# Strassen's seven half-size products in pairs of column blocks after the attention, with operand sums, and gates and branch results kept in DRAM

## The chip, the core and the metric

The kernel runs on one core of one Trainium2 chip. Its engines are TensorE (PE in the profile: matrix products), VectorE (DVE), ScalarE (ACT), GpSimd (POOL) and SyncE (SP, which here only starts DMAs). The metric is the device time of one launch in microseconds (us). The kernel before took 1020.76 us, the median of three runs (1018.58 to 1023.02).

## The reference

One layer on 1024 frames of 1024 channels, all in float32. Cut to what matters here:

```python
h = x @ w_in          # q, k, v, gate_a, alpha_low, pool_in, gate_b, merge_logits
o = gated_linear_attention(q, k, v, log_alpha)          # 4 heads, chunks of 64 frames
y_a = norm(o) * gla_norm_g * silu(gate_a)
y_b = pooled_and_mixed(pool_in, w_pool_grp) * pool_scale * silu(gate_b)
g_a, g_b = split(sigmoid(merge_logits + b_merge))
merged = g_a * (y_a @ w_proj_a) + g_b * (y_b @ w_proj_b)
return layernorm(ALPHA * x + merged @ w_out) * ln_g + ln_b
```

`pooled_and_mixed` takes, per group of 256 channels, a trailing mean over 2, 4, 8 or 16 frames minus the frame itself, and a 256 by 256 product. Every other product named here is 1024 deep.

## The kernel before, in words

**Products.** A float32 operand is held as an exact pair of two reduced-precision (fp32r) parts, hi and lo, and a product is hi·hi + hi·lo + lo·hi. `split` (L49) makes a pair: ACT casts hi (L50), DVE subtracts lo = src − hi (L51). A column block is 128 output columns for all 1024 frames: `acc_gen` (L101) runs 8 blocks of depth times 3 parts times 2 halves of 512 frames, 48 instructions of 128x512 (L112), into a PSUM tile of two banks (`ps_acc`, two such tiles). The weights of a block come in one 512 KB load into `raw` and are split in two pieces of 128x512.

**Stages.** After the loads come the v, q, k and decay products, then the attention, head after head (L470 to L515). Between the attention's steps `fill` (L453) runs products that do not depend on it; the last of them are the eight blocks of the merge logits of branch A (`la`), whose raw results go to DRAM (`la_d`). From then on the order is that of the code: per pool group two `pi` blocks (the pooling input), two `gb` blocks (the gate) and a small mix `mx`; then `lb` (merge gate b) and `pb` (projection b) in turn; then `gta` (gate a, times the attention's output, read back from DRAM); then `pa` (projection a, gated, plus branch B's result `mb`); then `out` (L638, the product with w_out), the residual and the layernorm. Each is eight column blocks, `out` eight frame blocks in two halves. The operands stay in SBUF: x (`xh`, `xl`), y_b and later y_a (`yh`, `yl`), merged (`mh`, `ml`), w_out (`wo0`, `wo1`), the gates and `mb`.

**What sets the order.** Each engine runs its own queue in order and waits for the others by semaphores. The queues follow the order in which the code issues the work; a block under `tc.high_priority(offset=...)` is placed that much earlier. All DMAs of this kernel are started from SP's one queue, and a DMA that waits holds up those behind it there. A tile of a pool waits until the earlier user of its buffer is done.

**Who does what after the attention.** PE runs the products. DVE makes the lo parts, the gating products (L565, L579, L593, L613), the pooling sums, the residual and the layernorm. ACT makes the hi parts, the gates and PSUM copies. POOL does eight additions of `mb` (L614) and the power of the layernorm's root (L415).

## Time and profile before

| | us |
|---|---|
| median of three runs | 1020.76 |
| profiled execution, first to last instruction (span) | 1019.1 |
| PE busy | 993.6 |
| DVE busy | 498.5 |
| ACT busy | 287.9 |
| POOL busy | 111.7 |

The profiled execution's own time is told by its span; the median of the runs lies 1.7 us above that, which is taken as what lies around the span. PE is busy 98% of it. The stages after the attention begin in the trace at 378.7 us (`pi`, `gb`, `mx`), 575.2 (`lb`, `pb`), 749.1 (`gta`), 836.2 (`pa`) and 923.2 (`out`); the last product ends at 1011. "Idle before" in a group of instructions is the time the engine stood still ahead of them, and the name behind the arrow is what it then waited for.

### The profile page before, as it was taken

Reading aid. Unit: us, or ns where it says so; the run is one execution under the profiler, and the core shown is the slowest. Engines: PE = TensorE matmul, PEld = TensorE weight load, DVE = VectorE, ACT = ScalarE, POOL = GpSimd, SP = SyncE. Lnnn points to the kernel's source line nnn. Section 1 sums busy time; section 2 is a strip of 40 time slices with the busy share of each in tenths; the row PEclk is TensorE's granted clock in tenths of the full one; section 3 lists DMA queues with packets and bytes.
Section 4 is the critical chain, followed back from the end, with each engine's and each line's share of the span. In section 5 each row is a group of like instructions: output and inputs, shape, how many; then the busy total and the mean of one; then the engine's idle time right before and its main releaser. Section 6 shows DMA issues by size and latency. Waiting matters only on the chain.

```text
span 1019.1 us, 12386 instructions
## 1 busy us (share of the span) xinstructions
PE 993.6 (98%) x5104; PEld 821.8 (81%) x5104; DVE 498.5 (49%) x743; ACT 287.9 (28%) x471; POOL 111.7 (11%) x56
## 2 busy tenths in 40 slices
...
GB/s 296 49 27 33 27 90 28 78 89 62 39 71 88 81 114 65 68 27 68 26 68 27 124 48 57 42 43 60 42 53 109 76 87 102 133 93 210 68 62 104
DMA packets 61353, 77.34 MB, mean 76 GB/s; under 512 B 40128, under 2 KB 42432, under 8 KB 61296
## 3 DMA queue, kind: packets, MB, share of 16 engines
...
q14 instruction: 17, 0.14, 0.0%
...
## 4 chain that ended last, share of the span: by engine, by line
PE 85%; DVE 9%; issue 2%; ACT 1%; POOL 1%; DMA 1%; SPq 0%; DVEq 0%; ACTq 0%; POOLq 0%
PE ps_gb L112 9%; PE ps_pi L112 9%; PE ps_lb L112 9%; PE ps_pa L112 9%; PE ps_gta L112 9%; PE ps_pb L112 9%; PE ps_v L146 8%; PE ps_la L112 8%; PE ps_out L638 5%; PE ps_q L112 4%; PE ps_mx L112 2%; PE ps_k L112 2%; PE ps_o L401 1%; PE ps_s L364 1%; PE ps_o L403 1%
## 5 line engine op out<-in xcount | busy, mean ns | idle before, releaser
L614 POOL TENSOR_TENSOR m<-m,mb 128x1024 f32<-128x1024 f32 x8 | 20.4, 2550 | 549.0 <-DVE m L613 549.0
L638 PE MATMUL ps_out<-wo,mh 128*128 128x512 f32 (+1 forms) x272 | 79.8, 376 | 0.0
L353 POOL TENSOR_TENSOR ks<-k,e 128x1024 f32<-128x1024 f32 x20 | 56.9, 2848 | 84.1 <-ACT e L349 59.5
L638 PEld LDWEIGHTS ps_out<-wo,mh 128*128 128x128 f32 x272 | 50.1, 188 | 9.4
L112 PE MATMUL ps_la<-xl,whi_la 128*128 128x512 f32 x128 | 51.2, 400 | 0.0
L638 PE MATMUL ps_out<-wo,ml 128*128 128x512 f32 (+1 forms) x136 | 51.2, 377 | 0.0
L112 PE MATMUL ps_la<-xh,wlo_la 128*128 128x512 f32 x128 | 51.1, 399 | 0.0
L112 PE MATMUL ps_la<-xh,whi_la 128*128 128x512 f32 x128 | 50.8, 397 | 0.0
L112 PE MATMUL ps_gb<-xl,whi_gb 128*128 128x512 f32 x128 | 49.8, 389 | 0.0
L112 PE MATMUL ps_pi<-xl,whi_pi 128*128 128x512 f32 x128 | 49.8, 389 | 0.0
L112 PE MATMUL ps_gb<-xh,wlo_gb 128*128 128x512 f32 x128 | 49.8, 389 | 0.0
L112 PE MATMUL ps_gb<-xh,whi_gb 128*128 128x512 f32 x128 | 49.8, 389 | 0.0
L112 PE MATMUL ps_pi<-xh,wlo_pi 128*128 128x512 f32 x128 | 49.8, 389 | 0.0
L112 PE MATMUL ps_pi<-xh,whi_pi 128*128 128x512 f32 x128 | 49.8, 389 | 0.0
L112 PE MATMUL ps_lb<-xl,whi_lb 128*128 128x512 f32 x128 | 49.8, 389 | 0.0
L112 PE MATMUL ps_lb<-xh,whi_lb 128*128 128x512 f32 x128 | 49.8, 389 | 0.0
L112 PE MATMUL ps_lb<-xh,wlo_lb 128*128 128x512 f32 x128 | 49.8, 389 | 0.0
L112 PE MATMUL ps_pb<-yh,whi_pb 128*128 128x512 f32 x128 | 49.8, 389 | 0.0
L112 PE MATMUL ps_pb<-yl,whi_pb 128*128 128x512 f32 x128 | 49.8, 389 | 0.0
L112 PE MATMUL ps_pb<-yh,wlo_pb 128*128 128x512 f32 x128 | 49.8, 389 | 0.0
L112 PE MATMUL ps_gta<-xh,whi_gta 128*128 128x512 f32 x128 | 49.8, 389 | 0.0
L112 PE MATMUL ps_gta<-xl,whi_gta 128*128 128x512 f32 x128 | 49.8, 389 | 0.0
...
## 6 DMA issues: line engine op xcount, KB each, us to landing
oT<-oTs SPq DMA_DIRECT2D x32, 128.0 KB, 2.2
raw_la<-in_w_blk SPq DMA_DIRECT2D x8, 512.0 KB, 3.8
la<-la SPq DMA_DIRECT2D x8, 512.0 KB, 5.0
raw_pi<-in_w_blk SPq DMA_DIRECT2D x8, 512.0 KB, 3.5
raw_gb<-in_w_blk SPq DMA_DIRECT2D x8, 512.0 KB, 3.5
raw_lb<-in_w_blk SPq DMA_DIRECT2D x8, 512.0 KB, 3.4
raw_pb<-in_w_pb SPq DMA_DIRECT2D x8, 512.0 KB, 3.4
oTl<-oT SPq DMA_DIRECT2D x32, 128.0 KB, 4.0
```

Of the source, the lines that this page charges most:

```text
L112: pe.matmul(o, lhsT=a[:, k, :], rhs=b[k][:, sl], start=(i == 0), stop=(i == n - 1))
L146: pe.matmul(o, lhsT=a[k][:, ts], rhs=w[b][:, k - k0, :], start=(k == 0 and i == 0), stop=(k == KB - 1 and i == 2))
L353: pool_e.tensor_tensor(out=ks, in0=kt_[h], in1=e, op=ALU.mult)
L364: pe.matmul(psv[c * CH:c * CH + CH, b, :], lhsT=ks[:, cs], rhs=qs[:, cs], start=True, stop=True)
L401: pe.matmul(po, lhsT=pt[:, b, :], rhs=v[b][:, hs], start=True, stop=(b == 0))
L403: pe.matmul(po, lhsT=d["qi"][:, b * P:b * P + P], rhs=d["st"][:, b - 1, :], start=False, stop=True)
L614: pool_e.tensor_tensor(out=m, in0=m, in1=mb[j], op=ALU.add)
L638: pe.matmul(ps, lhsT=a[k][:, tb * P:tb * P + P], rhs=wo[k][:, b, c0:c1], start=(k == 0 and i == 0), stop=(k == KB - 1 and i == 2))
```

## The change

After the attention the seven kinds of 1024-deep products (the last two `la` blocks apart) are taken in pairs of column blocks. A pair is a product of a weight matrix A (256 columns, 1024 deep) and an operand B (1024 deep, 1024 frames), each cut in four quarters, and is computed by Strassen's scheme in Winograd's form as 7 products of half the depth, half the columns and half the frames: 7 times 12 instructions of 128x512 in place of 8 times 12. There are 28 pairs: `pi0` to `gb3` in turn, `lb0` to `lb3`, `gta0` to `gta3`, `pb0` to `pb3`, `pa0` to `pa3` and `o0` to `o3`. In `out` the roles change: w_out is the operand B and rows of `m` are the weights.

- **Weight sums** (`Pair.prep`): four of the seven weights are sums of quarters, made on POOL (L634, 128x512), then split on ACT and DVE. This runs three products ahead of PE (`AHEAD`), in a ring of four.
- **Operand sums** (`Operands`): four of the seven operands (T1 to T4) are sums of quarters of B. Their quarters are loaded from DRAM into `c4` (eight buffers of 512 KB, shared by all results), summed (L567: T3 and T4 on DVE, T2 and T1 on POOL; each in two pieces of 128x1024) and split (`close`, also two pieces each). For x three unsummed operands are already there; y_b (`YB`), y_a (`YA`) and w_out (`WO`) need all seven. The steps for an operand are issued between the seven products of the last pair of the stage before: `YB` in `gta3`, `YA` in `pb3`, `WO` in `pa3`. Those of x are issued ahead of `la6`.
- **Combining the products** (`Pair.product`): u and e (L668, L670) and three of the four outputs add a PSUM bank and an SBUF tile on DVE. PSUM has banks a, b, c, d (2, 1, 2, 1 buffers) and two for the mix.
- **Results in DRAM**: the gates b, y_b, y_a, `mb` and `m` are stored as they come and loaded where they are needed. In `pb` and `pa` three of four gating products move to POOL (L907), and so does the addition of `mb` (L909, in halves). In `out` the rows of `m` are loaded in pieces of 64 KB (L930), and three of four additions into z are on POOL (L960).
- **Attention**: six of the eight `la` blocks are left to `fill` (`LA_FILL`); `la6` and `la7` follow it.

The core of the diff:

```diff
-                      z_gen(3), q_gen(3), k_gen(3)] + [la_gen(j, sg) for j in range(8)])
+                      z_gen(3), q_gen(3), k_gen(3)] + [la_gen(j, sg) for j in range(LA_FILL)])
...
+    class Operands:
+        def load(self, q):
+            got = [piece(f"{self.nm}q{q}_{g}") for g in range(2)]
+            for g in range(2):
+                with tc.high_priority(offset=60):
+                    self.fetch(got[g], q, g)
+            self.q[q] = got
+        def close(self, o, q):
+            pool = op_b if o[0] == "T" else op_a
+            self.ops[o] = [pool.tile([P, 4, 512], F32R, tag="op", name=f"{self.nm}{o}{n}") for n in "hl"]
+            for g in range(2):
+                split(self.q[q][g], *(t[:, 2 * g:2 * g + 2, :] for t in self.ops[o]))
+        def sum(self, q, a, b, op, eng):
+            for g in range(2):
+                eng.tensor_tensor(out=self.q[q][g], in0=self.q[a][g], in1=self.q[b][g], op=op)
...
+    PRODUCTS = [("1", "B11", "a", True), ("7", "T3", "c", True), ("6", "T2", "b", True), ("5", "T1", "d", True),
+                ("2", "B21", "a", False), ("4", "T4", "c", False), ("3", "B22", "d", False)]
...
+            src = {"1": lambda: q("11"), "2": lambda: q("12"), "4": lambda: q("22"),
+                   "7": lambda: total(q("11"), q("21"), ALU.subtract),
+                   "6": lambda: total(q("22"), self.s["7"], ALU.subtract),
+                   "5": lambda: total(q("21"), q("22"), ALU.add),
+                   "3": lambda: total(q("12"), self.s["6"], ALU.subtract)}[p]()
...
+            for k in range(4):
+                ks = slice(k * P, k * P + P)
+                for x, y in ((whi, bh), (whi, bl), (wlo, bh)):
+                    pe.matmul(self.ps[b], lhsT=x[:, ks], rhs=y[:, k, :], start=(first and n == 0), stop=(n == 11),
...
+            if p == "6":
+                dve.tensor_tensor(out=self.u, in0=ps["b"], in1=self.u, op=ALU.add)
+                self.e = post.tile([P, 512], F32, tag="e", name=f"e_{self.nm}", bufs=1)
+                dve.tensor_tensor(out=self.e, in0=ps["c"], in1=self.u, op=ALU.add)
...
+                dve.tensor_tensor(out=t, in0=ps, in1=more, op=ALU.add)
+                pool_e.tensor_tensor(out=o, in0=t, in1=o, op=ALU.mult)
+            if more_d:
+                pool_e.tensor_tensor(out=o, in0=o, in1=mb[i][:, hs_[half]], op=ALU.add)
+            sp.dma_start(out_d[j0 + i][:, hs_[half]], o)
...
+            dve.scalar_tensor_tensor(out=o, in0=o, scalar=ALPHA, in1=ps, op0=ALU.mult, op1=ALU.add)
+            if more is not None:
+                pool_e.tensor_tensor(out=o, in0=o, in1=more, op=ALU.add)
+            dve.bn_stats(out=st[t][:, half, :], in_=o)
```

**Order, first place.** DVE's queue at the end of the attention, in the kernel before: `rsa_o3` and `rst_o3` belong to the last head's norm, whose eight scalings of `v` and eight transposes then follow.

```order
L414 TENSOR_SCALAR rsa_o3_2922<-ss_3_2824 128x8
L51 TENSOR_TENSOR wlo_la7_3017<-raw_la7_3015,whi_la7_3016 128x512 x2
L416 TENSOR_TENSOR rst_o3_2924<-rsr_o3_2923 128x8
L417 TENSOR_TENSOR rst_o3_2924<-rst_o3_2924,rsa_o3_2922 128x8
L418 TENSOR_SCALAR rst_o3_2924<-rst_o3_2924 128x8
L419 TENSOR_TENSOR rsr_o3_2923<-rsr_o3_2923,rst_o3_2924 128x8
L428 SCALAR_TENSOR_TENSOR v_0_89<-v_0_89,rsr_o3_2923,gn_3_2931 128x256
```

And now, from the last two of those transposes on; `xq22` and `xq12` are quarters of x, `xT3l` is the lo part of an operand sum.

```order
L431 STREAM_TRANSPOSE oTs_3_1_2973<-v_6_106 128x256
L431 STREAM_TRANSPOSE oTs_3_1_2973<-v_7_107 128x256
L54 TENSOR_TENSOR wlo0_la6_3100<-raw_la6_3095,whi0_la6_3099 128x512
L54 TENSOR_TENSOR wlo1_la6_3104<-raw_la6_3095,whi1_la6_3103 128x512
L54 TENSOR_TENSOR wlo0_la7_3112<-raw_la7_3097,whi0_la7_3111 128x512
L54 TENSOR_TENSOR wlo1_la7_3116<-raw_la7_3097,whi1_la7_3115 128x512
L567 TENSOR_TENSOR xq22_0_3051<-xq22_0_3051,xq12_0_3055 128x1024
L54 TENSOR_TENSOR xT3l_3062<-xq22_0_3051,xT3h_3061 128x1024
L567 TENSOR_TENSOR xq22_1_3052<-xq22_1_3052,xq12_1_3056 128x1024
```

The weight of the first product behind the attention, which stood ahead of the norm and the transposes, stands behind them, and the operand sums of x behind it.

**Order, second place.** POOL's queue from `pa` to `out`, before: the last two additions of `mb` and the first roots.

```order
L614 TENSOR_TENSOR m_6_6381<-m_6_6381,mb_6_5217 128x1024
L614 TENSOR_TENSOR m_7_6453<-m_7_6453,mb_7_5335 128x1024
L415 TENSOR_TENSOR rsr_ln0_6783<-rsa_ln0_6782,mhalf_82 128x1
L415 TENSOR_TENSOR rsr_ln1_6824<-rsa_ln1_6823,mhalf_82 128x1
L415 TENSOR_TENSOR rsr_ln2_6865<-rsa_ln2_6864,mhalf_82 128x1
```

And now, in the last pair of `pa`: `woq` are quarters of w_out, `gpa3` the pair's results, `S7_o0` and `S6_o0` weight sums of the first pair of `out`.

```order
L567 TENSOR_TENSOR woq12_0_7158<-woq12_0_7158,woq11_0_7127 128x1024
L567 TENSOR_TENSOR woq22_0_7154<-woq22_0_7154,woq11_0_7127 128x1024
L634 TENSOR_TENSOR S7_o0_7357<-raw_o0_0_7317,raw_o0_1_7326 128x512
L567 TENSOR_TENSOR woq12_1_7159<-woq12_1_7159,woq11_1_7128 128x1024
L567 TENSOR_TENSOR woq22_1_7155<-woq22_1_7155,woq11_1_7128 128x1024
L907 TENSOR_TENSOR gpa3_1_7217<-tpa3_11_7222,gpa3_1_7217 128x512
L909 TENSOR_TENSOR gpa3_1_7217<-gpa3_1_7217,mbpa3_1_7220 128x512
L909 TENSOR_TENSOR gpa3_0_7247<-gpa3_0_7247,mbpa3_0_7250 128x512
L907 TENSOR_TENSOR gpa3_1_7217<-tpa3_10_7277,gpa3_1_7217 128x512
L909 TENSOR_TENSOR gpa3_1_7217<-gpa3_1_7217,mbpa3_1_7220 128x512
L907 TENSOR_TENSOR gpa3_0_7247<-tpa3_01_7302,gpa3_0_7247 128x512
L909 TENSOR_TENSOR gpa3_0_7247<-gpa3_0_7247,mbpa3_0_7250 128x512
```

Twelve POOL additions and products now stand where two stood, four of them 128x1024.

**Order, third place.** SP's queue between `pa` and `out`, before: the last loads of w_out, then the residual's x.

```order
L601 DMA rwo1_6_6496<-in_w_o 128x512
L668 DMA lng_6509<-in_ln_g 128x1024
L669 DMA lnb_6510<-in_ln_b 128x1024
L601 DMA rwo1_7_6501<-in_w_o 128x512
L632 DMA z_0_6663<-in_x 128x1024
```

And now: `m_6` and `m_7` are stored in halves, `raw_o0_0` and `raw_o0_1` are the rows of `m` that are the weights of pair `o0`, `z` is x for the residual.

```order
L910 DMA m_7_3038<-gpa3_1_7217 128x512
L937 DMA lng_7446<-in_ln_g 128x1024
L910 DMA m_6_3037<-gpa3_0_7247 128x512
L937 DMA lnb_7448<-in_ln_b 128x1024
L941 DMA z_4_7450<-in_x 128x1024
L941 DMA z_0_7490<-in_x 128x1024
L930 DMA raw_o0_0_7317<-m_7_3038 128x128
L930 DMA raw_o1_0_7335<-m_7_3038 128x128
L941 DMA z_5_7642<-in_x 128x1024
L941 DMA z_1_7682<-in_x 128x1024
L941 DMA z_6_7834<-in_x 128x1024
L930 DMA raw_o0_1_7326<-m_6_3037 128x128
```

The last piece of the first pair's weights stands behind five loads into `c4` buffers, of which `z_1` and `z_6` take the buffers of the last w_out quarters and so wait until these are split.

## Rows read from the trace of the kernel before

**Rows 1.** The page's first part: busy us, share of the span, instructions.

```profile
PE 993.6 (98%) x5104; PEld 821.8 (81%) x5104; DVE 498.5 (49%) x743; ACT 287.9 (28%) x471; POOL 111.7 (11%) x56
```

**Rows 2.** Busy time by stage after the attention; each stretch, its length, then busy (instructions).

```profile
378.70:575.00 196.30, 196.30 (x864) 162.01 (x863) 88.38 (x114) 58.47 (x101) 0.00 (x0) 1.00 0.16 51
749.30:836.40 87.10, 87.10 (x386) 72.12 (x386) 28.65 (x31) 24.39 (x32) 0.00 (x0) 1.00 0.40 85
836.40:923.40 87.00, 87.00 (x385) 72.08 (x384) 44.00 (x39) 32.40 (x42) 18.00 (x7) 1.00 0.34 106
923.40:1010.00 86.60, 86.60 (x403) 72.57 (x402) 50.62 (x98) 4.75 (x8) 13.03 (x8) 1.00 0.31 113
```

**Rows 3.** Tile `ps_gta`: duration ns min/median/max, first and last start in us.

```profile
L112 PE MATMUL ps_gta<-xh,whi_gta x128: 389/389/389, 749.3 to 835.7; 128*128 128x512 f32 x128
L112 PE MATMUL ps_gta<-xh,wlo_gta x128: 389/389/389, 749.8 to 836.2; 128*128 128x512 f32 x128
```

**Rows 4.** Groups by line and form: busy us, mean ns of one, idle before.

```profile
L51 DVE TENSOR_TENSOR wlo_gta<-raw_gta,whi_gta 128x512 fp32r<-128x512 f32 x16 | 10.4, 688 | 45.6 <-ACT whi_gta L50 45.6
L51 DVE TENSOR_TENSOR ml<-m,mh 128x1024 fp32r<-128x1024 f32 x8 | 9.8, 1226 | 6.1 <-ACT mh L50 6.1
L645 DVE BATCH_NORM_STATS2 bst<-z 128x6 f32<-128x512 f32 x15 | 10.2, 690 | 0.3
L644 DVE SCALAR_TENSOR_TENSOR z<-z,ps_out 128x512 f32<-128x512 f32 x15 | 10.1, 680 | 22.9 <-PE ps_out L638 22.9
L415 POOL TENSOR_TENSOR rsr_ln<-rsa_ln,mhalf 128x1 f32<-128x1 f32 x8 | 11.6, 1451 | 74.1 <-DVE rsa_ln L414 74.1
```

**Rows 5.** Tile `m`: duration ns min/median/max, first and last start in us.

```profile
L614 POOL TENSOR_TENSOR m<-m,mb x8: 2402/2526/2712, 853.9 to 925.5; 128x1024 f32<-128x1024 f32 x8
```

**Rows 6.** DVE and POOL from 852 to 859 us: start, duration, instruction.

```profile
853.59 3.49 DVE L51 TENSOR_TENSOR wlo_pa<-raw_pa,whi_pa 128x512 fp32r<-128x512 f32 x2
857.64 1.23 DVE L51 TENSOR_TENSOR ml<-m,mh 128x1024 fp32r<-128x1024 f32 x1 [0.57 <-ACT mh L50]
858.79 0.69 DVE L51 TENSOR_TENSOR wo<-rwo,wo 128x512 fp32r<-128x512 f32 x1
...
853.89 2.64 POOL L614 TENSOR_TENSOR m<-m,mb 128x1024 f32<-128x1024 f32 x1 [495.38 <-DVE m L613]
```

**Rows 7.** DVE and POOL from 126 to 130 us.

```profile
126.72 1.23 DVE L352 TENSOR_TENSOR qs<-q,e 128x1024 f32<-128x1024 f32 x1 [0.23 <-ACT e L349]
127.87 0.42 DVE L406 COPY v<-ps_o 128x256 f32<-128x256 f32 x1
128.86 0.42 DVE L406 COPY v<-ps_o 128x256 f32<-128x256 f32 x1 [0.57 <-ACT ps_o L407]
...
126.77 3.42 POOL L353 TENSOR_TENSOR ks<-k,e 128x1024 f32<-128x1024 f32 x1 [4.22 <-ACT e L349]
```

**Rows 8.** DVE at the end of the attention, 355 to 368 us.

```profile
354.63 0.42 DVE L406 COPY v<-ps_o 128x256 f32<-128x256 f32 x1 [4.21 <-PE ps_o L403]
...
357.60 1.30 DVE L51 TENSOR_TENSOR wlo_la<-raw_la,whi_la 128x512 fp32r<-128x512 f32 x2 [0.80 <-ACT whi_la L50]
...
362.78 2.72 DVE L435 STREAM_TRANSPOSE oTs<-v 128x256 f32<-128x256 f32 x8
```

**Rows 9.** Stretches in the attention; the granted clock stands third from the end.

```profile
105.00:109.60 4.60, 1.04 (x28) 0.89 (x26) 4.60 (x5) 2.18 (x4) 1.25 (x1) 1.00 0.00 0
109.60:116.40 6.80, 5.96 (x25) 5.01 (x26) 6.80 (x12) 0.45 (x1) 2.34 (x1) 0.50 0.14 40
```

**Rows 10.** DMA issues: count, KB each, median us from issue to landing.

```profile
oT<-oTs SPq DMA_DIRECT2D x32, 128.0 KB, 2.2
raw_gta<-in_w_blk SPq DMA_DIRECT2D x8, 512.0 KB, 3.5
```

**Rows 11.** DVE's first residual after PE's last product.

```profile
1011.20 0.41 DVE L644 SCALAR_TENSOR_TENSOR z<-z,ps_out 128x256 f32<-128x256 f32 x1
```

More of the change, by code (lines that the diff above doesn't have):

```diff
@@ new lines, in run @@
+    def run(items):
+        flat = [(it, i) for it in items for i in range(it.n)]
+        items[0].load()
+        at = {id(it): n for n, it in enumerate(items)}
+        for n in range(len(flat) + AHEAD):
+            if n < len(flat):
+                it, i = flat[n]
+                if i == 0 and at[id(it)] + 1 < len(items):
+                    items[at[id(it)] + 1].load()
+                it.prep(i)
+            if n >= AHEAD:
+                it, i = flat[n - AHEAD]
+                it.product(i)
@@ new lines, in la_plain, with use @@
+    def la_plain(j):
+        t = []
+        def use(half, ps):
+            if not half:
+                t.append(c4.tile([P, S], F32, tag="c", name=f"la_{j}"))
+            act.copy(t[0][:, half * 512:half * 512 + 512], ps)
+            if half:
+                sp.dma_start(la_d[j], t[0])
+        return Plain(f"la{j}", blk(w_blk, 32 + j), use)
+    for j in range(LA_FILL, KB):
+        items.append(la_plain(j))
+    yb_d = [d_tile(f"yb_{j}") for j in range(KB)]
+    ya_d = [d_tile(f"ya_{j}") for j in range(KB)]
@@ new lines, in encoder_layer, with outs_of, get, add_or_copy @@
+    gb_d = [d_tile(f"gb_{j}") for j in range(KB)]
+    m_d = [d_tile(f"m_{j}") for j in range(KB)]
+    mb_d = [d_tile(f"mb_{j}") for j in range(KB)]
+    hs_ = (lo_half, hi_half)
+    def outs_of(nm):
+        t = {}
+        def get(i):
+            if i not in t:
+                t[i] = c4.tile([P, S], F32, tag="c", name=f"{nm}_{i}")
+            return t[i]
+        return get
+    def add_or_copy(out, ps, more):
+        if more is None:
+            act.copy(out, ps)
+        else:
+            dve.tensor_tensor(out=out, in0=ps, in1=more, op=ALU.add)
@@ new lines, in pool_pair, with use, pooled @@
+    def pool_pair(gi):
+        u, ph, pl = outs_of(f"u{gi}"), [], []
+        def use(i, half, ps, more):
+            add_or_copy(u(i)[:, hs_[half]], ps, more)
+        def pooled():
+            win = WINDOWS[gi]
+            for jj in range(2):
+                j = 2 * gi + jj
+                cur, w = u(jj), 1
+                while w < win:
+                    nxt = c4.tile([P, S], F32, tag="c", name=f"s_{j}_{w}")
+                    dve.tensor_tensor(out=nxt[:, w:], in0=cur[:, w:], in1=cur[:, :S - w], op=ALU.add)
+                    act.copy(nxt[:, :w], cur[:, :w])
+                    cur, w = nxt, 2 * w
+                dve.tensor_tensor(out=cur[:, :16], in0=cur[:, :16], in1=rcnt[:, gi, :], op=ALU.mult)
+                dve.scalar_tensor_tensor(out=cur, in0=cur, scalar=1.0 / win, in1=u(jj), op0=ALU.mult, op1=ALU.subtract)
+                ph.append(c4.tile([P, S], F32R, tag="c", name=f"ph_{j}"))
+                pl.append(c4.tile([P, S], F32R, tag="c", name=f"pl_{j}"))
+                split(cur, ph[jj], pl[jj])
+        return Pair(f"pi{gi}", blk(w_blk, 16 + 2 * gi), X, use, pooled), (ph, pl)
@@ new lines, in gate_pair, with use @@
+    def gate_pair(nm, j0, operands, func, then, bias=None, hooks=()):
+        t = outs_of(nm)
+        def use(i, half, ps, more):
+            o = t(i)[:, hs_[half]]
+            kw = {} if bias is None else dict(bias=bm_t[:, bias + i:bias + i + 1])
+            if more is None:
+                act.activation(o, ps, func, **kw)
+            else:
+                dve.tensor_tensor(out=o, in0=ps, in1=more, op=ALU.add)
+                act.activation(o, o, func, **kw)
+        return Pair(nm, blk(w_blk, j0), operands, use, lambda: then(t), hooks)
```

454 lines of the change are left out of this document (280 added, 174 removed).

## The prediction

> **What bounds the kernel now.** I read the page's totals first: TensorE is busy 98% of the span, DVE 49%, POOL 11% [rows 1]. Then the busy time by stage: after the attention PE stands at the full length of every stretch at the full clock, while DVE is busy 88 of 196 us, 29 of 87, 44 of 87 and 51 of 87, and POOL does nothing until 836 us [rows 2]. So each product removed there is worth its pitch. That is read from one stage: the 384 products of gta start at 749.3 and the last at 836.2 [rows 3], 86.9 / 383 = 0.2269 us each.
>
> Next I asked who could become the bound. What matters is whether DVE and POOL can work at the same time, since the change gives both much more. From 853.59 two lo parts of 128x512 took DVE 3.49 us, while POOL's addition ran from 853.89 to 856.53 [rows 6]. Two such lo parts alone take 1.30 [rows 8], the addition alone 2.40 [rows 5]: together 3.70 if one waits for the other, 2.64 if they overlap. 3.49 is the first. The other way round POOL waits: `ks` took 3.42 us when DVE's product of two SBUF tiles started 0.05 us ahead of it [rows 7]. DVE's copies out of PSUM ran in their usual 0.42 us inside that same POOL instruction [rows 7]. So POOL additions and DVE operations on two SBUF tiles take turns; DVE operations with a PSUM source do not take part.
>
> The Trainium skill ("SBUF — State Buffer", section on the two separate sides) states this as a rule: a GpSimd operation and a DVE operation with two SBUF inputs share one pair of ports under an exclusive lock, and the loser is blocked for the whole instruction. The trace agrees (3.49 against 3.70). By the rule the sums below add up; without it the first rival would be the forecast.
>
> **The gain.** 28 pairs times 12 instructions are 336 products less, at 0.2269 us: 76.2 us. Nothing else on PE goes. This is full only where the operands are there in time.
>
> **Prices of what is added.** A lo part of 128x512 on DVE 0.65 (half of 1.30 [rows 8]); a DVE operation of 128x1024 on SBUF tiles 1.15, the distance of two starts (857.64 and 858.79 [rows 6]); a POOL addition of 128x1024 2.40 [rows 5]. One of 128x512 is not in the trace; it lies between 1.20 (half of that) and 2.40 (as long), and I take 1.20, since DVE's 128x512 takes 0.69 against 1.23 [rows 4]. Additions from PSUM 0.68, like the residual's [rows 4].
>
> Counted over the order after the attention, DVE gets 200 weight splits (130 us), 58 closes of operands and pooled inputs (67) and 68 other operations of 128x1024 (78); POOL gets 164 additions of 128x512 (197 us) and 16 of 128x1024 (38). These take turns: 510 us, against 2,544 products (28 x 84 of the pairs, 96 of la6 and la7, 96 of the mix) or 577 us of PE. As a mean that fits. By stage it does not: a pair of lb has 7 x 0.65 + 4 x 1.20 = 9.4 us in 19.06 us of PE (84 x 0.2269), but the operand sums are lumped into one pair each, and cannot start earlier. So I went through the stages; t counts from a stage's first product.
>
> 1. *End of the attention.* The last product of the heads ends at about 354.6, where DVE's copy of it starts [rows 8]; call it T. Before, the split of the next la weight ran at 357.6, ahead of the transposes that end at 365.5 [rows 8]. Now it stands behind them, and PE has 15 products (3.4 us) left: it idles from T+3.4 to about T+11.5, 8 us. Behind that come la6, la7 and two products of pi0, so without any wait the third would start at T+31.3. Up to its operand T2 DVE has 10 operations of 128x1024 and 3 splits (13.5), POOL 4 large and 3 small additions (13.2), 26.7 us in turns. The quarters are loaded on SP behind the transposes' stores (2.2) and behind each other (3.5 each [rows 10]), so the first sum starts at about T+21 and T2 is there at T+47.7. Loss 16.4, the 8 included. Bounds: 8 and 21.
> 2. *Pool groups.* Two pairs and the mix (43.5 us of PE) hold about 29 us in turns and some 10 of other DVE work in one chain. 3, from 0 to 10.
> 3. *y_b, in gta3 and pb0.* 18 large DVE operations and 10 splits (27.2), 4 large and 9 small POOL additions (20.4): 47.6 us, from t = 10, when the first quarters can be there, so t = 57.6. PE, which takes products of pb1 ahead meanwhile, needs the last operand after 193 products, at 43.8. Loss 14, from 4 to 18.
> 4. *y_a, in pb3 and pa0.* 14 large DVE operations and 9 splits (22.0), 2 large and 7 small POOL additions (13.2): 35.2 us from t = 5.4, so 40.6, needed at 34.7. 6, from 0 to 10.
> 5. *w_out, in pa3 and o0.* 16 large DVE operations and 4 splits (21.0), 4 large and 8 small POOL additions (19.2): 40.2 us from t = 3.4, so 43.6. Only then do the loads of z get their buffers, behind which the last rows of m for pair o0 stand on SP. Their load (2.2 at least [rows 10]), a POOL sum, a cast and a split make it about t = 47.5. PE has pa3 and two products of o0, 24.5 us. Loss 23, from 10 to 28. Before, nothing waited here.
> 6. *out.* A pair: 7 splits (4.6), 4 layernorm passes (4.6), 7 POOL additions (8.4), 17.6 in turns; two powers of 1.45 [rows 4] in DVE's chain make it 20.5, against 19.06. 7 in four pairs with fringes, from 0 to 12.
> 7. *Tail.* From the first residual behind the last product, at 1011.20 [rows 11], to the end there are now 7.9 us. A whole row in one piece, a second norm and a POOL addition beside it: 3, from 0 to 6.
> 8. *Clock.* After a stretch with PE busy 1.04 of 4.6 us the granted clock was 0.50 for 6.8 us, that is 1.2 GHz [rows 9]. A product there takes twice as long, so a dip costs up to 3.4 us. Four long waits; PE is partly late anyway just behind them. 5, from 0 to 12.
>
> Sum of losses: 16.4 + 3 + 14 + 6 + 23 + 7 + 3 + 5 = 77.4. Span 1019.1 - 76.2 + 77.4 = 1020.3; with 1.7 around it as the median of the runs has it, 1022. The other traffic hides: ACT's casts and gates stay far below PE's time, and the added DRAM traffic of gates and results runs beside products, but for the loads named.
>
> **The rivals.**
>
> *A: the lumps are absorbed.* The queues have slack ahead of the transitions (in lb and most of gta and pb half the time) and PE takes products of the next pair ahead of the late one. Then the lower ends hold: 8 + 0 + 4 + 0 + 10 + 0 + 2 + 2 = 26, that is 1020.8 - 76.2 + 26 = 971; up to 1005 for mixtures. For it: DVE 49% and POOL 11% busy [rows 1]. Against: a quarter's load needs a buffer of the shared eight, so the sums cannot run ahead into the slack. The extreme of it is that DVE and POOL overlap for these forms: then only the 8 at T, some 6 at o0 and the tail stay, 962. Rows 6 speak against it.
>
> *B: the steps are a chain as well.* An operand goes load, POOL or DVE sum, ACT cast, DVE lo part, and every queue is in order, so there are moments in which neither DVE nor POOL works. The four transitions hold 26.7 + 47.6 + 35.2 + 40.2 = 150 us in turns, which I took as gapless. If a fifth of it is idle, 30 us more are lost: 1052. It makes the kernel slower from 4 us on, 3% of the 150. For it: ml starts 0.57 us after DVE came free, waiting for its cast [rows 6]. Against: there are two pieces per sum, so one can go while the other is cast.
>
> *C: the 128x512 additions on POOL cost more than half,* say 1.45 as the power does. Then 164 of them take 41 us more, of which those in the transitions and in out (27 + 28 of them, at 0.25 each 14 us) show: 1036.
>
> **How the numbers follow.** A measurement of this kernel can tell about 0.5% from no change, so 1015.7 to 1025.9 is the same. The forecast with its own range, 1008 to 1034, gets 0.45: 0.10 of it below 1015.7, 0.21 within, 0.14 above. A gets 0.28, all faster. B gets 0.19 and C 0.08, all slower. Together faster 0.38, same 0.21, slower 0.41. The range that should hold the time 8 times in 10 goes from 976, the lower part of A, to 1048, most of B; the likeliest is 1022.
>
> **What would show it right or wrong.** In the profile after, PE should be busy about 917 us of 1020, with its gaps at four places: behind the heads' last product (8 us, then 9 more before pi0's third product), in pb0, at pa0, and the longest in o0 behind its second product, ended by the POOL sum that needs the last rows of m. DVE and POOL together, PSUM sources left out, should be without gaps there; if they have gaps, it is B, and if PE has none, A. POOL's 128x512 should read 1.2 us alone and up to 1.9 beside DVE. The clock should dip behind each of these gaps. If the gap in o0 is ended by something other than m's rows, my fifth step is wrong; if the 510 us in turns come out well under that, the prices are.

## The result and the profile after

The changed kernel takes 1057.77 us (median of four runs, 1053.78 to 1059.69) against 1021.09 for the kernel before, run beside it on the same chip: a ratio of 1.0354, interval 1.0328 to 1.0381. It is 3.5% slower. The forecast was 1022 with a range of 976 to 1048, so the time lies above the range. The profiled execution has a span of 1055.0 us, 35.9 more than before.

The page's first part, which answers to [rows 1], and the clock in 40 slices:

```profile
PE 948.3 (90%) x4744; PEld 770.6 (73%) x4744; DVE 744.9 (71%) x984; ACT 381.9 (36%) x630; POOL 397.3 (38%) x228
...
PEclk9999899998998998999999999999699889877997
```

The products are gone as the change says, and the share of TensorE fell from 98% to 90%: the span grew though the work shrank. The stretches after the attention, in the columns of [rows 2] (the granted clock stands third from the end), show where:

```profile
378.70:410.00 31.30, 23.48 (x94) 17.93 (x93) 26.64 (x16) 12.38 (x18) 19.43 (x8) 0.92 0.39 148
423.80:578.80 155.00, 155.00 (x685) 128.37 (x684) 117.09 (x145) 57.23 (x107) 44.37 (x28) 1.00 0.22 73
655.00:731.00 76.00, 76.00 (x337) 62.93 (x336) 47.70 (x57) 32.27 (x50) 24.00 (x15) 1.00 0.71 189
731.00:767.00 36.00, 26.79 (x87) 19.44 (x86) 33.87 (x28) 16.59 (x22) 21.87 (x11) 0.76 0.60 162
806.00:860.00 54.00, 43.32 (x168) 34.12 (x168) 46.60 (x43) 26.33 (x33) 34.51 (x18) 0.87 0.63 214
904.00:935.00 31.00, 25.72 (x104) 20.71 (x103) 26.55 (x19) 11.56 (x14) 21.96 (x11) 0.89 0.50 151
935.00:961.20 26.20, 0.66 (x4) 0.24 (x2) 14.17 (x12) 7.38 (x8) 11.00 (x7) 0.61 0.84 293
961.20:1041.00 79.80, 73.54 (x312) 59.15 (x312) 67.28 (x111) 16.72 (x28) 45.23 (x31) 0.98 0.26 86
```

Inside the stages PE is as full as it was: 155.0 us of 155.0 in the pool groups, 76.0 of 76.0 in `gta`. The time goes where a stage changes its operand: 378.7 to 410 (x), 731 to 767 (y_b), 806 to 860 (y_a), 904 to 961 (w_out). The five longest waits of PE behind the attention (start, duration, instruction, idle before and what ended it):

```profile
369.92 0.80 PE L713 MATMUL psa_la<-xh,wlo_la 128*128 128x512 f32 x1 [5.91 <-DVE wlo_la L54]
...
406.24 0.80 PE L660 MATMUL psb_pi<-xT2h,whi_pi 128*128 128x512 f32 x1 [6.44 <-ACT whi_pi L53]
...
846.15 0.77 PE L660 MATMUL psd_pa<-yaT1h,whi_pa 128*128 128x512 f32 x1 [6.67 <-DVE tpb L906]
...
921.98 0.77 PE L660 MATMUL psc_pa<-yaT4h,whi_pa 128*128 128x512 f32 x1 [5.28 <-DVE e_pa L670]
...
961.12 0.80 PE L660 MATMUL psb_o<-woT2h,whi_o 128*128 128x512 f32 x1 [25.54 <-ACT whi_o L53]
```

The first product behind each wait takes up to 0.80 us, twice its usual 0.39: that is the clock of 1.2 GHz. Around the wait in o0 the granted clock stood at 0.50 (third from the end):

```profile
941.00:964.50 23.50, 3.38 (x7) 2.33 (x8) 12.99 (x12) 6.04 (x9) 8.49 (x5) 0.50 0.74 260
```

To turn this into a sum I took, for each stage, the time between its first product and the next stage's, less its products times 0.2269 us (the forecast's pitch). T is here the start of the heads' last product, 0.4 us ahead of the end that the forecast calls T. A wait that is given without its row is counted in the same way, from start to start, and reads some 0.2 us longer than the idle time in a row (25.7 against 25.54 in o0). The lines are good to about 0.2 us.

| step of the forecast | forecast, us | measured, us |
|---|---|---|
| T itself | 0 | 4.0 (358.2 against 354.2) |
| 1 end of attention, x | 16.4 | 21.5 (2.0 + 8.6 in la6, 10.9 in pi0) |
| 2 pool groups | 3 | 0 |
| 3 y_b | 14 | 16.8 |
| 4 y_a | 6 | 16.2 (pb3 3.8, pa0 12.4) |
| in no step: pb1, pb2, pa2 | 0 | 6.1 |
| 5 w_out, o0 | 23 | 35.7 (pa3 8.0, o0 27.7) |
| 6 out | 7 | 6.9 |
| 7 tail | 3 | 6.0 |
| 8 clock | 5 | 17.9, held in the lines above |
| sum | 77.4 | 113.2 |
| gain | 76.2 | 76.2 |

113.2 - 76.2 is 37.0; of the 1.1 above the 35.9, 0.6 is what the kernel before lost itself by the same count, and the rest is rounding and the pitch, which reads 0.2267 in the stretches without a wait. The clock's 17.9 is what all pitches between 0.2269 and 0.51 us have above 0.2269; some 16 of it lie where the granted clock was 0.50.

**Do POOL and DVE take turns?** DVE and POOL in `pa3`, as [rows 6] showed them for before:

```profile
924.46 0.68 DVE L906 TENSOR_TENSOR tpa<-psd_pa,e_pa 128x512 f32<-128x512 f32 x1
925.06 3.01 DVE L54 TENSOR_TENSOR woT2l<-woq,woT2h 128x1024 fp32r<-128x1024 f32 x1
928.00 1.78 DVE L54 TENSOR_TENSOR wlo_o<-raw_o,whi_o 128x512 fp32r<-128x512 f32 x1
929.71 2.30 DVE L54 TENSOR_TENSOR woT1l<-woq,woT1h 128x1024 fp32r<-128x1024 f32 x1
...
924.62 2.38 POOL L567 TENSOR_TENSOR woq<-woq,woq 128x1024 f32<-128x1024 f32 x1 [1.16 <-DVE woT3l L54]
926.94 2.29 POOL L907 TENSOR_TENSOR gpa<-tpa,gpa 128x512 f32<-128x512 f32 x1
```

A lo part of 128x1024 takes 1.21 us alone and 3.01 beside a POOL sum of 2.38; it begins 0.44 us after the sum and ends about 1.1 after the sum's end, its own time. Then the POOL product takes 2.29, of which it stood 1.1 behind that lo part. DVE's addition from PSUM (924.46) started ahead of POOL's sum and kept its 0.68. In the whole trace no such addition (L668, L670, L821, L906) took more than 0.692, though 52 of the 116 started inside a POOL operation.

**The chain in o0.** DVE, then POOL, then SP, ahead of the 25.5 us wait:

```profile
948.37 2.35 DVE L54 TENSOR_TENSOR woB22l<-woq,woB22h 128x1024 fp32r<-128x1024 f32 x2
961.10 2.78 DVE L54 TENSOR_TENSOR wlo_o<-S_o,whi_o 128x512 fp32r<-128x512 f32 x2 [10.38 <-ACT whi_o L53]
...
944.10 2.13 POOL L909 TENSOR_TENSOR gpa<-gpa,mbpa 128x512 f32<-128x512 f32 x1
959.15 1.26 POOL L634 TENSOR_TENSOR S_o<-raw_o,S_o 128x512 f32<-128x512 f32 x1 [12.92 <-DMA raw_o<-m]
...
946.26 0.32 SPq L910 DMA_DIRECT2D m<-gpa  x1
946.62 0.43 SPq L937 DMA_DIRECT2D lnb<-in_ln_b  x1
947.34 1.46 SPq L941 DMA_DIRECT2D z<-in_x  x2
948.90 0.93 SPq L930 DMA_DIRECT2D raw_o<-m  x2
949.88 1.61 SPq L941 DMA_DIRECT2D z<-in_x  x3
951.99 0.33 SPq L930 DMA_DIRECT2D raw_o<-m  x1
```

PE's last product ahead of the wait starts at 935.19. Until 946.2 POOL still works on `pa3`'s results. Then 12.9 us pass in which the last half of `m` is stored (946.26), five loads of z are issued ahead of the last 64 KB of o0's weights (951.99), and these land 7.1 us later. Only then can POOL make `S_o`. DVE has been done with w_out since 950.7.

**Bank d in pa0.** DVE's queue while PE waits 6.67 us for it:

```profile
840.72 1.21 DVE L54 TENSOR_TENSOR yaB22l<-yaq,yaB22h 128x1024 fp32r<-128x1024 f32 x1
841.86 0.68 DVE L54 TENSOR_TENSOR wlo_pa<-S_pa,whi_pa 128x512 fp32r<-128x512 f32 x1
842.46 1.21 DVE L567 TENSOR_TENSOR yaq<-yaq,yaq 128x1024 f32<-128x1024 f32 x1
843.59 1.21 DVE L54 TENSOR_TENSOR yaB22l<-yaq,yaB22h 128x1024 fp32r<-128x1024 f32 x1
844.73 0.68 DVE L54 TENSOR_TENSOR wlo_pa<-raw_pa,whi_pa 128x512 fp32r<-128x512 f32 x1
845.33 0.68 DVE L906 TENSOR_TENSOR tpb<-psd_pb,u_pb 128x512 f32<-128x512 f32 x1
```

`tpb` reads pb3's last result out of bank d, whose product ended at 829.0. DVE has no gap, but works through the y_a steps ahead of it; bank d has one buffer, so pa0's fourth product waits, though its operand T1 is there (its last lo part ends at 832.3).

**The tail.** The last product starts at 1040.54. The row that answers to [rows 11], the POOL addition behind it, and the last pass:

```profile
1042.34 0.67 DVE L958 SCALAR_TENSOR_TENSOR z<-z,psd_o 128x512 f32<-128x512 f32 x1
...
1043.09 1.26 POOL L960 TENSOR_TENSOR z<-z,u_o 128x512 f32<-128x512 f32 x1 [1.40 <-DVE z L958]
...
1050.00 1.28 DVE L949 SCALAR_TENSOR_TENSOR z<-z,rsr_ln,lnb 128x1024 f32<-128x1024 f32 x1
```

From 1040.54 to the end are 14.5 us, 6.0 more than before: the last row's residual waits behind the other row's statistics, and a POOL addition and a second norm follow.

### The profile page after: what moved, and what is told of

It is laid out like the page before. It is cut to its first block, busy times and chain, and to the rows that moved or that the text cites. A ratio compares the mean times of both kernels' runs of the same rounds, so it can differ in the third digit from the quotient of the medians.

```text
span 1055.0 us, 12966 instructions
## 1 busy us (share of the span) xinstructions
PE 948.3 (90%) x4744; PEld 770.6 (73%) x4744; DVE 744.9 (71%) x984; ACT 381.9 (36%) x630; POOL 397.3 (38%) x228
## 4 chain that ended last, share of the span: by engine, by line
PE 57%; DVE 17%; issue 8%; POOL 7%; DMA 6%; ACT 2%; SPq 1%; POOLq 0%; DVEq 0%; ACTq 0%
PE ps_v L142 8%; PE ps_la L119 6%; PE ps_q L119 2%; PE psd_pi L660 2%; PE psc_gta L660 2%; PE psa_lb L660 2%; PE psa_gta L660 2%; PE psd_lb L660 2%; PE psd_gb L660 2%; PE psc_gb L660 2%; PE psc_lb L660 2%; PE ps_mx L841 2%; PE psa_gb L660 2%; PE psd_gta L660 2%; PE psc_pi L660 2%
## 5 line engine op out<-in xcount | busy, mean ns | idle before, releaser
L142 PE MATMUL ps_v<-whi_v,xh 128*128 128x264 f32 x128 | 37.7, 297 | 0.1
L142 PE MATMUL ps_v<-wlo_v,xh 128*128 128x264 f32 x128 | 37.6, 298 | 0.0
L142 PE MATMUL ps_v<-whi_v,xl 128*128 128x264 f32 x128 | 37.3, 292 | 0.0
L360 PEld LDWEIGHTS ps_s<-qs,ks 128*64 128x64 f32 x640 | 23.0, 141 | 14.5 <-issue 14.3
L348 DVE TENSOR_TENSOR qs<-q,e 128x1024 f32<-128x1024 f32 x20 | 30.0, 1500 | 2.4 <-ACT e L345 2.3
L360 PE MATMUL ps_s<-qs,ks 128*64 128x64 f32 x640 | 27.5, 231 | 3.2 <-DVE qs L348 2.2
L660 PE MATMUL psb_o<-woT2h,whi_o 128*128 128x512 f32 x16 | 7.1, 445 | 25.5 <-ACT whi_o L53 25.5
L907 POOL TENSOR_TENSOR gpb<-tpb,gpb 128x512 f32<-128x512 f32 x12 | 22.1, 1842 | 18.8 <-DVE tpb L906 16.1
L380 PE MATMUL ps_st<-v,ket 128*128 128x256 f32 x56 | 19.0, 473 | 11.3 <-DVE st L385 11.3
L403 ACT ACTIVATE ps_o<-v 128x256 f32<-128x256 f32 x32 | 12.4, 387 | 44.2 <-DVE v L402 44.1
L119 PE MATMUL ps_k<-xl,whi_k 128*128 128x512 f32 x64 | 26.8, 419 | 0.0
L909 POOL TENSOR_TENSOR gpa<-gpa,mbpa 128x512 f32<-128x512 f32 x16 | 24.7, 1550 | 5.2 <-DMA mbpa<-mb 4.4
L119 PE MATMUL ps_k<-xh,whi_k 128*128 128x512 f32 x64 | 26.1, 408 | 0.0
L119 PE MATMUL ps_k<-xh,wlo_k 128*128 128x512 f32 x64 | 26.1, 407 | 0.0
```

Of the source, the lines that this page charges most:

```text
L119: pe.matmul(o, lhsT=a[:, k, :], rhs=mov(b, k, half), start=(i == 0), stop=(i == n - 1))
L142: pe.matmul(o, lhsT=sta(a, k, tb), rhs=w[b][:, k - k0, :], start=(k == 0 and i == 0), stop=(k == KB - 1 and i == 2))
L348: dve.tensor_tensor(out=qs, in0=qt[h], in1=e, op=ALU.mult)
L360: pe.matmul(psv[c * CH:c * CH + CH, b, :], lhsT=ks[:, cs], rhs=qs[:, cs], start=True, stop=True)
L380: pe.matmul(pst, lhsT=d["ket"][:, b, :], rhs=v[b][:, hs], start=True, stop=True)
L660: pe.matmul(self.ps[b], lhsT=x[:, ks], rhs=y[:, k, :], start=(first and n == 0), stop=(n == 11), skip_group_check=not first)
```

## The experiments

Times are medians with the ratio to the kernel before on the same chip. "After" is the changed kernel, 1057.77. Losses by stage come from one trace per run; where a stage and what feeds it are the same, they differ by about 1 us between traces (pi0 lost 10.9 to 12.0 in after and experiments 3, 4, 6, 7 and 9).

**1. The operand sums T1 and T2 on DVE** (L583, L587).

```diff
-                self.sum("22", "22", "11", ALU.add, pool_e)
+                self.sum("22", "22", "11", ALU.add, dve)
```

> Edit: the operand sums T1 and T2 (8 halves of 128x1024 on POOL per operand set, 16 in all) go to DVE; nothing else. Theory (POOL additions and DVE operations on two SBUF tiles take turns): each sum costs 1.15 us of the shared time in place of 2.40, 5.0 us less in each of the four operand transitions; PE waits behind them shorten by about that, and two dips of the clock may go: 15 to 20 us faster than the changed kernel, about 1038 to 1043. Rival 1 (they overlap): DVE gets 4.6 us more in each transition, 10 to 18 us slower, about 1068 to 1075. Rival 2 (the waits come from late loads and chains, not from the sum of work): no change within 3 us.

Measured 1041.43 (1.0195 [1.0166, 1.0225]), as the theory of turns has it: giving DVE more work, in its busiest stretches, gained 16 us. The loss in pi0 fell from 10.9 to 5.1 us. The time alone would also fit a chain in which only the sum itself got shorter; that the two engines block each other is shown by the rows of `pa3` above.

**2. All additions and products of POOL after the attention on DVE** (L583, L587, L634, L907, L909, L960).

```diff
-                pool_e.tensor_tensor(out=t, in0=a, in1=b, op=op)
+                dve.tensor_tensor(out=t, in0=a, in1=b, op=op)
...
-                pool_e.tensor_tensor(out=o, in0=t, in1=o, op=ALU.mult)
+                dve.tensor_tensor(out=o, in0=t, in1=o, op=ALU.mult)
```

> Edit: every POOL addition and product behind the attention (16 operand sums, 112 weight sums, 24 gating products, 16 additions of mb, 12 additions into z) goes to DVE; POOL keeps the powers. Theory (turns): the shared time falls by 164 x (1.27 - 0.65) + 16 x 1.25 = 120 us, while DVE's PSUM work, some 127 us that ran beside POOL, now stands in one line with it. By stage: x 7 us less, y_b 9, y_a 12, pa's later pairs 10, w_out 6 less, out about 9 more (23 us of DVE per pair against 19.06 of PE): 1020 to 1030. Rival (POOL's work was beside DVE's and hidden): DVE gets 125 us more on a stretch in which it is already 71% busy: over 1090.

Measured 1031.47 (1.0098 [1.0068, 1.0127]). Its page and two rows of `pa0`:

```profile
PE 936.7 (91%) x4744; PEld 763.2 (74%) x4744; DVE 761.3 (74%) x1164; ACT 382.4 (37%) x630; POOL 91.6 (9%) x48
```

```profile
834.16 0.69 DVE L906 TENSOR_TENSOR tpb<-psd_pb,u_pb 128x512 f32<-128x512 f32 x1
...
835.00 0.77 PE L660 MATMUL psd_pa<-yaT1h,whi_pa 128*128 128x512 f32 x1 [10.38 <-DVE tpb L906]
```

DVE took 180 instructions more and was busy only 16 us longer (761.3 against 744.9), since its own no longer wait: the work on two engines was not beside each other but in turns, and POOL's share of it at half the speed (a 128x512 sum 1.26 us alone there, 0.69 on DVE). What stays is the order of the queue: the wait for bank d is now 10.4 us, and o0's wait 28.4. No run reads bank d ahead of the steps, so what that alone would give is not shown.

The Trainium skill ("SBUF — State Buffer", section "SBUF: two separate sides") gives the lock as the only contention of the engines' ports in SBUF. The trace of after agrees in so far as DVE's additions out of PSUM stay at 0.69 us or less, also beside POOL. That the page's list is complete no run here shows.

**3. Only the gates, `mb` and z additions on DVE** (L907, L909, L960).

```diff
-                pool_e.tensor_tensor(out=o, in0=t, in1=o, op=ALU.mult)
+                dve.tensor_tensor(out=o, in0=t, in1=o, op=ALU.mult)
```

> Edit: only the gating products, the additions of mb and those into z go from POOL to DVE (52 operations of 128x512); operand and weight sums stay. Theory (a pa pair holds 11 POOL operations of 1.27 and 7 splits of 0.65, 18.5 us in turns for 19.06 us of PE, so it cannot make up what y_a's transition left late; this is the term the prediction left out): a pa pair comes to 14 us in turns, the 12.9 us lost in the third and fourth pa pair and a part of the 16 at y_a go: 10 to 16 us faster than the changed kernel, 1042 to 1048. Rival (the losses in pa come from the late loads of its weights): 0 to 4 us faster, 1054 to 1058.

Measured 1053.76 (1.0334 [1.0309, 1.0358]): the theory missed by 6 us, and no change against after can be told, as the rival has it. `o1` to `o3` lose nothing now (6.9 before), but the waits in `pa2` and `pa3` grew (losses 5.9 and 11.3). POOL there, ahead of `pa2`:

```profile
873.98 1.30 POOL L634 TENSOR_TENSOR S_pa<-raw_pa,raw_pa 128x512 f32<-128x512 f32 x1 [12.94 <-DMA raw_pa<-in_w_pa]
```

POOL stands free for 12.94 us; what is late is the load of the weights.

**4. z, ln_g and ln_b loaded behind o0's last rows of m.** A one-column ACT copy from `raw` into the tile holds each of these loads back.

```diff
+            mark.append(post.tile([P, 1], F32, tag="mark", name="mark", bufs=1))
+            act.copy(mark[0], raw[:, 6 * P:6 * P + 1])
+        act.copy(t[:, :1], mark[0])
```

> Edit: the loads of z and of the layernorm's g and b wait (by a one-column copy on ACT) until the last rows of m for pair o0 have landed. Theory: in the changed kernel the last piece of the weights of o0 was issued behind seven loads of 512 KB and landed 7.1 us later, when DVE had been idle 10.4 us; alone it takes 2 to 3 us, so o0's 25.7 us wait shrinks by 4 to 6 us, of which part may come back as a wait for z: 2 to 6 us faster, 1052 to 1056. Rival (that load is slow for itself, being 128 rows of 512 bytes from DRAM just written): no change, and the load still takes 7 us.

Measured 1051.08 (1.029 [1.026, 1.032]). The wait in o0 fell from 25.7 to 17.9 us. POOL there:

```profile
953.16 1.26 POOL L634 TENSOR_TENSOR S_o<-raw_o,S_o 128x512 f32<-128x512 f32 x1 [5.24 <-DMA raw_o<-m]
```

POOL's wait for the rows is 5.24 instead of 12.92 us: the difference is the z loads ahead in the queue.

**5. Experiments 2 and 4 together.**

> Edit: both e2 (all additions on DVE) and e3 (loads of z and of g and b behind the last rows of m). Theory: in e2 the wait in o0 is 28.4 us, ended by those rows; e3 cut 7.8 of such a wait: 1023 to 1026. If the wait in o0 is then ended by the close of w_out's operands on DVE, less: 1026 to 1030.

Measured 1025.65 (1.0042 [1.0022, 1.0061], eight runs), as expected. The two gains of 26 and 7 us add up to within 1 us. At this point the change costs 0.4% instead of 3.5.

**6. `out` as plain products, the rest as after.** w_out's quarters are split without sums, o0 to o7 take 96 products each.

```diff
-    run([out_pair(tb) for tb in range(4)])
+    run([out_flat(tb) for tb in range(NT)])
```

> Edit: the product with w_out is computed plainly (8 frame blocks of 48 products, w_out's four quarters split without sums, the rows of m still loaded from DRAM); all else as changed. Theory (the out stage loses more to its operand sums than Strassen saves there): 48 products, 10.9 us, come back; the 27.7 us lost in o0 shrink to about 8 (rows of m alone), the 6.9 lost in o1 to o3 and part of the 8 in pa3 go: 15 to 22 us faster than the changed kernel, 1036 to 1043. Rival (what holds o0 is the late store and reload of m behind the loads of z): the wait stays at 15 or more and the kernel stays within 5 us, 1052 to 1060.

Measured 1034.13 (1.0128 [1.0086, 1.0171]), a little better than expected: it gains 23.6 us over after though four pairs give up 10.9 us of products, so 34.5 of losses went. The first block of `out` still waits 9.4 us for `m`.

**7. No operand steps for y_b, y_a and w_out** (the pairs use x's operands, so the kernel leaves out part of the layer's work and its result is not the layer's).

```diff
-        items.append(gated(f"pa{q}", 2 * q, YA, w_pa, gate_a, mb_d, m_d, WO.steps() if q == 3 else ()))
+        items.append(gated(f"pa{q}", 2 * q, X, w_pa, gate_a, mb_d, m_d, ()))
```

> Leaves out the operands of pb, pa and out (loads, sums and splits of y_b, y_a and w_out): these pairs multiply by the operands of x, all else stays. Theory (what is lost after gta is the operand transitions): of the 102 us lost behind the heads' last product those of y_b (18), y_a (16) and w_out (8 in pa3, about 15 in o0) go, and part of pa's: 50 to 60 us faster, 998 to 1008. Rival (the additions and gates of pb, pa and out on POOL, and the DRAM traffic, hold the pairs themselves): waits in every pb and pa pair, 1025 or more.

Measured 1003.28 (0.9826 [0.9777, 0.9875]). So the operand steps cost some 54 us of the 113 (two runs, 5.6 us apart). From `pb0` to `pa1` nothing is lost; but o0:

```profile
904.33 0.80 PE L660 MATMUL psb_o<-xT2h,whi_o 128*128 128x512 f32 x1 [14.85 <-ACT whi_o L53]
```

Even with DVE and POOL free of operand steps, o0 waits 14.9 us: that is `m` on its way through POOL's product and addition, the store, the load, the weight sum and the cast. The store took part of it by waiting in SP's queue: POOL's addition ended at 891.8, the store was issued at 895.2.

**8. A fourth buffer for raw weights** (`t` gives up its own buffer and shares that of `e`).

```diff
+                odd = pairs_seen[0] % 2 and i
+                pool, tag = (ring, "raw1") if odd else (wraw, "raw")
+                t = pool.tile([P, 1024], F32, tag=tag, name=f"raw_{self.nm}_{i}", bufs=1 if odd else 3)
```

> Edit: a fourth buffer for the raw weights of the pairs (the gates' scratch tile shares e's buffer to make room), so that both loads of the next pair stand ahead of the stores of m in SP's queue. Theory (after the run e9: pa3's weights are loaded late, because the fourth block's load waits for a buffer and then stands behind stores of m that wait for the gates): the waits of 3.4 and 5.7 us ahead of the sixth product in the last pairs of pa shrink to under 2 each, 5 to 10 us faster than the changed kernel, 1047 to 1053. Rival (they are the turns of POOL and DVE in pa): the same two waits stay, within 3 us of it, and then both are needed.

Measured 1047.38 (1.0263 [1.0212, 1.0315]). What it was to mend is this, in the chain of waits of after (start, us, what), and on DVE and PE:

```profile
883.50 3.40 DMA m<-gpa
...
886.96 0.38 SPq L880
...
887.95 4.96 DMA raw_pa<-in_w_pa
...
893.07 1.42 POOL S_pa L634
```

```profile
889.26 1.23 DVE L54 TENSOR_TENSOR woB11l<-woq,woB11h 128x1024 fp32r<-128x1024 f32 x1 [3.54 <-ACT woB11h L53]
...
895.77 0.47 PE L660 MATMUL psc_pa<-yaT4h,whi_pa 128*128 128x512 f32 x1 [3.05 <-DVE e_pa L670]
```

On SP a load of w_out (886.96) waits for a `c4` buffer, which is free when a store of `m` has landed (883.50 + 3.40). The next pair's raw weights stand behind that load, and POOL's sum behind their 4.96 us. DVE in turn waits with a lo part of w_out, and `e_pa`, which PE needs, is queued behind it. With the fourth buffer the loss in `pa2` is 1.1 instead of 4.9, and `pa3` still waits 2.3 us, above the 2 expected. But of the 10 us that the run gains, `pa2` to o0 give only 2.6: o0's wait grew as the earlier ones went. About 4 came in `pb0` (where POOL had waited 13.6 us for raw weights in after) and 4.2 in `o1` to `o3`.

**9. The stores of `mb` and `m` on ACT's queue** (L910).

```diff
-            sp.dma_start(out_d[j0 + i][:, hs_[half]], o)
+            act.dma_start(out_d[j0 + i][:, hs_[half]], o)
```

> Edit: the stores of mb and m are issued from ACT's queue, so that SP's loads no longer stand behind a store that waits for a gating product. Theory: as with a fourth buffer, the two waits in the last pairs of pa shrink, and quarters of y_a and w_out come earlier: 4 to 10 us faster, 1047 to 1053. Rival: the store now holds up ACT's casts in the same way, 0 to 10 us slower, 1057 to 1068.

Measured 1055.79 (1.0346 [1.0271, 1.042]), no change that can be told, and neither the theory's 1047 to 1053 nor the rival's 1057 to 1068. `pa3` lost 1.3 instead of 8.0, and o0 33.5 instead of 27.7: together 34.8 against 35.7. This fits a wait ahead of o0 that is hidden behind the one in o0, whose end is set by the w_out steps and the way of `m`; how much of o0's longer wait comes from stores that hold up ACT's casts, as the rival has it, the run does not separate.

**10. pi0 as two plain blocks.**

```diff
+        if gi == 0:
+            blocks_, p = pi0_plain()
+            items.extend(blocks_)
```

> Edit: the first pair (pi0) is computed plainly, 96 products on the operands of x that are already there, so that the operand sums of x are first needed by gb0. Theory: the wait of 10.7 us in pi0 goes and 12 products (2.7 us) come: 7 to 9 us faster, about 1050. The 8 us wait ahead of la6 stays. Rival (the sums of x then delay the splits of the plain blocks as well, since DVE and POOL stand in one line): 0 to 4 us faster.

Measured 1056.86 (1.0346 [1.0314, 1.0379]), no change that can be told. The rival was right: the wait moves to the second block (4.7 us), whose split stands behind x's sums on DVE. Needing an operand later helps only if the queue's order is changed too.

**11. Strassen's pairs for the products with x alone**; `pb`, `pa` and `out` plain, T1 and T2 of x on DVE.

```diff
+    for j in range(KB):
+        items.append(gated_flat(f"pb{j}", j, YB, w_pb, lambda t, j: sp.dma_start(t, gb_d[j]), None, mb_d, ya_steps.get(j)))
```

> Edit: Strassen for the 16 pairs on x alone (pi, gb, lb, gta), its operand sums on DVE; pb, pa and out plain, with operands split ahead of their stage and the addition of mb on DVE; results still via DRAM. Theory: 192 products less than before, 43.6 us; the x transition costs about 16, the attention's end comes 2.5 later, out's start about 8, the tail about 3: 1021 - 43.6 + 29.5 = 1007, from 1000 to 1012; faster than both. Rival (traffic via DRAM, with loads of 64 KB and the stores, is itself a cost wherever it is used): waits in pb, pa and out as well, 1020 or more.

Measured 1007.10 (0.9862 [0.9832, 0.9891]), as expected. `pb` and `pa` run at 21.76 us per 96 products, without a gap. One set of operand sums is paid for 16 pairs (43.6 us of products) here; y_b and y_a serve four pairs each (10.9 us).

**12. The same, all eight `la` blocks inside the attention, pi0 plain with its splits ahead of the sums.**

```diff
-LA_FILL = 6
+LA_FILL = 8
...
+            with tc.high_priority(offset=HPRI if self.operands is None else 0):
+                split(self.raw[:, i * 512:i * 512 + 512], hi, lo)
```

> Edit on e6: all eight la blocks run in the attention's filler again (LA_FILL 8), and pi0 is plain with its splits ahead of the operand sums, so that la6 and la7 cover the norm and the transposes, and pi0 the operand sums of x. Theory: of e6's 16 us lost between the heads' last product and gb0 2 to 4 stay, 2.7 come for the 12 products more, and the attention's end comes back to 354: 1007 - 12 - 2.7 = 992, from 989 to 998. Rival (as in the run with pi0 plain alone, the splits are held up behind the sums): 1003 to 1007.

Measured 996.02 (0.976 [0.9735, 0.9785]). The sum of losses behind T is about 12 us in the trace, which is of the fastest of the four runs (991.57).

**13. And the first two `out` blocks run their depths 0 to 6 ahead of 7**, as the kernel before did with six blocks.

```diff
+            for ks in (range(KB - 1), (KB - 1,)):
+                for t, o in enumerate(self.o):
```

> Edit on e10: the first two frame blocks of out run their depths 0 to 6 ahead of depth 7, so that the rows of m from pa's last block are needed 19 us later. Theory: the 9 us lost at out's start in e6 are the reload of m's last rows; they go: 7 to 9 us faster than e10, 983 to 990. Rival (what is late there are the splits of w_out or the loads of z): no change against e10.

Measured 990.75 (0.972 [0.9703, 0.9736]): it beats both kernels, the one before by 2.8%. The gain over experiment 12 is 5.3 us, less than the 7 to 9 expected, since o0 lost 5.5 there and not 9; in this run o0 loses nothing. Its page:

```profile
PE 956.5 (97%) x4900; PEld 785.8 (80%) x4900; DVE 606.9 (61%) x908; ACT 335.2 (34%) x563; POOL 183.0 (19%) x108
```

About 5.5 us are lost behind T; it keeps 15 of the 28 pairs, 180 products or 40.8 us.

## Why the prediction was wrong, point by point

The mechanism stands. The gain is 76.2 us as forecast, the stretches without a wait are exactly at the pitch, and the losses sit at the places named, the longest in o0. The turns of POOL and DVE hold (experiments 1 and 2). Wrong are sizes of terms, nearly all to one side, and in step 4 also what PE waits for. Of the signs that the prediction named, POOL's 128x512 sum read 1.26 us alone as said, but up to 2.3 beside DVE, not 1.9. PE was busy 948.3 us and not about 917: 5 of the 31 us lie ahead of T, and the slow products are in the rest.

- *Step 1* (16.4, measured 21.5, and T 4.0 late). The first product on T2 came at T+48.0, forecast T+47.7. But the first sum began at 382.24, T+24 and not T+21 (x's quarters took 8.0 us in the median, not 3.5), which shorter work made up. What PE had to do until then was overstated: 131 products, 29.7 us, lay ahead of it, since 11 of la were left at T and not 15. The forecast subtracted 31.3, and its own parts (15 + 96 + 24 products) make 30.6. That is 1.6 of the excess; about 3 came behind T2, in products at half clock and shorter waits. T itself was not in the sum. It lay between 355.4 and 358.3 in the runs with `LA_FILL` at 6 and at 353.1 and 356.7 with 8 (experiments 12 and 13), so it moves from trace to trace; 1.8 of the 4.0 stand already at the attention's first product (86.9 us against 85.2; 86.5 to 88.6 in the experiments). The change keeps x in quarters, and so splits it at the start in pieces of at most 512 frames where it was up to 1024, which the forecast did not count; whether that makes the 1.8, and what makes the rest, no run shows.
- *Step 2* (3, measured 0). The queues run three products ahead, which absorbs it; rival A holds there.
- *Step 3* (14, measured 16.8). The last lo part of y_b ended at 768.9, t = 57.5, forecast 57.6. The other 2.8 us and more are the clock: 4.5 us of pb0's loss are slow pitches.
- *Step 4* (6, measured 16.2), the step that failed most for its size. The last lo part of y_a ended at 844.8, t = 39.2, forecast 40.6: the work was priced right. What failed is "needed at 34.7". PE was stopped not by y_a's last operand but by bank d, needed 36 products into pa0, at t = 19.06 + 8.2 = 27.2, and read by DVE only at t = 39.7, in its turn behind the steps. I had counted DVE's queue as work, not as an order in which the reader of a bank has a place. In experiment 7, without the steps, pa0 loses nothing.
- *Left out* (pa2, 4.9, and pa3's part). I had said that the added DRAM traffic hides beside products. The loads of weights and of w_out do not: three raw buffers for two per pair, and a queue in which a load that waits for a buffer, and so for POOL and a store, holds up the weights behind it (experiments 3 and 8). The pa weights landed 5.2 us behind their issue in the median, against 3.5 for those of gta before [rows 10]; how much of the lateness is order in the queue and how much is the added traffic itself, no run separates.
- *Step 5* (23, measured 35.7 with pa3's own wait). DVE was done with w_out at t = 47.8, POOL with `m` at 43.3, forecast 43.6 for both. The last rows of `m` were to be usable at about t = 47.5 and were at 58.2: the load was priced at 2.2 us, from the stores in the attention [rows 10], and took 7.1 behind z. Experiment 4 takes 7.8 back.
- *Steps 6 and 7* (7 and 3, measured 6.9 and 6.0). That step 6 meets its number is in part luck: with a fourth raw buffer (experiment 8) these pairs lose 2.7, so late weights, which it did not name, are in the 6.9; that turns are in it too fits experiment 3, where they lose nothing. In the tail the two rows of the last pair are normed one behind the other.
- *Step 8* (5, measured 17.9). I counted four long waits. There are more, and a wait of 1 to 7 us leaves slow products behind it too; they stand in the losses of the other lines.

*The rivals.* B comes nearest in time (1052) but not in kind: neither DVE nor POOL was busy for 2.1 of the 55 us from 712 to 767, 1.2 of 54 from 806 and 1.5 of 47 from 904, far under its fifth. With DVE's operations on PSUM left out, as the prediction's sign has it, these are 4.1, 5.2 and 2.7: still under it, but together 12 us, more than the 4 from which B makes the kernel slower, so B holds in a small part. Only at x is it more, 10.7 of 40, nearly all of it waiting for loads. C is not it either: a 128x512 sum alone takes 1.26 us with starts 1.22 apart (959.15 and 960.37 in o0), near the 1.20 taken. A holds inside the stages and at none of the transitions. The range was too narrow on top because every bound was drawn around one step, and none for a resource that no step named.
